# Where the modulation of layer 0's gate and of layer 1 is computed: between the blocks of layer 0's merge, or between the projections of its mLSTM stage

## The chip, the core and the metric

The kernel runs on one core of a Trainium2 chip. The metric is the device time of one execution in microseconds (us). The engines are TensorE (PE in the profile, PEld for its weight loads), VectorE (DVE), ScalarE (ACT), GpSimd (POOL) and SyncE (SP), whose queue issues all of this kernel's loads.

## The reference

Two layers of a diffusion backbone. Each layer norms its input and modulates it with shift, scale and gate, which come from a conditioning vector. It feeds the result to three token mixers and merges their outputs by gates computed from the same input.

```python
def layer_fwd(x, xc, c, c_ctx, ...):
    shift, scale, gate = jnp.split(jax.nn.silu(c) @ w_mod + b_mod, 3, axis=-1)
    shift_c, scale_c, gate_c = jnp.split(jax.nn.silu(c_ctx) @ w_mod + b_mod, 3, axis=-1)
    h = rms_norm(x, norm_g) * (1.0 + scale[:, None]) + shift[:, None]
    hc = rms_norm(xc, norm_g) * (1.0 + scale_c) + shift_c
    p = [h @ w for w in split_cols(w_in, IN_SIZES)]      # and pc from hc
    y_a = ssd_branch(...); y_b = diff_branch(...); y_c = mlstm_branch(...)
    def merge(ya, yb, yc, gates):
        g = jax.nn.sigmoid(gates).reshape(gates.shape[:-1] + (N_BRANCH, D_MODEL))
        mixed = (g[..., 0, :] * (ya @ w_branch[0]) + g[..., 1, :] * (yb @ w_branch[1])
                 + g[..., 2, :] * (yc @ w_branch[2]))
        return mixed @ w_out
    x_new = x + gate[:, None] * merge(y_a, y_b, y_c, p[13])
    xc_new = xc + gate_c * merge(yc_a, yc_b, yc_c, pc[13])
```

There are 256 latent and 256 context tokens, and D_MODEL is 1024. `w_mod` is 1024 x 3072 for each layer. All numbers are 32-bit floats.

## The kernel before

**Projections.** A weight matrix is streamed in granules of 512 rows by 256 columns (`granules`, lines 123 to 139). SP loads 512 KB into one of three `raw` buffers, ScalarE rounds it to `whi` (line 120), and VectorE subtracts to get the rest, `wlo` (line 82, called from `split`). Both have three buffers. Three products (hi x hi, hi x lo, lo x hi) add up in PSUM: `mm_tok` (lines 149 to 151, 256 columns to an instruction) for outputs in token layout, `proj_ch` (lines 180 to 182, 512 columns) for outputs in channel layout. The sums stand in three PSUM banks named `acc`. A `proj_ch` takes two of them, a `proj_tok` one for each pair of token tiles.

**Order.** The Tile framework puts each engine's instructions into an order before the kernel runs. It takes those that are ready in a simulated time line, by priority. Band 0 (loads, splits, evacuations) goes ahead of band 1 (the mixers), and that ahead of band 2 (projections, and the modulation here). Within a band the order of the program counts. On the chip every engine's order is fixed. A pool that is opened on the memory of a released pool waits for the last use of what lay there.

**Stages of a layer.** These are the norm, branch A (SSD), branch B (differential attention), branch C (mLSTM), the merge and the output projection. The mLSTM stage runs `ml_core(j)` for four heads (band 1). It is a chain over four chunks in two directions in which TensorE, ScalarE and VectorE hand small tiles to each other: `pw`, `nu` (line 1105), `dn` (lines 1106 to 1110), `kw`, `C` (line 1125). The projections `mo_proj`, `mz_proj` and `ml_proj` of this and the next heads give TensorE work between the steps. Layer 1 computes outputs for the latent tokens alone, and so has half of those projections.

**The merge** (lines 1247 to 1279) has three branches of four column blocks. Each of the twelve steps is a gate projection (`fg`, tanh into `tg`) and a branch projection (`fb`, gate times projection, added up in `mixed`). Ahead of each branch its tokens are transposed into `yh`, `yl`.

**The modulation.** Blocks 0 to 3 of layer 0 are made at the start, on TensorE. The two blocks of layer 0's gate and the six of layer 1 are made by `mod_block` (lines 266 to 307), 512 columns of `w_mod` at a time. Four loads of 512 KB go into three `wm` buffers. For each of the eight k-tiles and the two conditioning vectors there is a product and an addition: ScalarE multiplies and GpSimd adds for one vector, and for the other VectorE does both at once in five k-tiles and ScalarE with GpSimd (over `mtmp`) in two. The sums stand in `macc` (one buffer). VectorE folds the partitions by half into `modrow` (one buffer). The block's end, `tail`, is four products on TensorE into an `acc` bank (line 300) and one VectorE addition into `modc` (line 302). The list `later` holds the eight blocks. `start()` puts one block's products into the program. `background()` puts the oldest block's tail there and then starts the next. Two blocks are started ahead, and nine places between the mLSTM's parts call `background()`.

Of the kernel before, what the change touches and what calls it, by code (L numbers as in the profile page):

```python
# [10 lines left out]
F32R = mybir.dt.float32r  # L11
# [5 lines left out]
PSUM = bass.MemoryType.PSUM  # L17

D = 1024
P = 128  # L20
KT = D // P
NT = 4
# [12 lines left out]
def hybrid_backbone_kernel(ctx: ExitStack, tc: tile.TileContext, A, out, dbg=None):  # L35
# [4 lines left out]
    # ---- priority bands: 0 loads, splits and evacuations; 1 mixers; 2 projections  # L40
# [52 lines left out]
    def bc(ap, n):  # L93
        """append a broadcast free dim of n"""
        return ap.unsqueeze(len(ap.shape)).to_broadcast(list(ap.shape) + [n])

    # ---- constants
# [20 lines left out]
    # ---- weight stream: granules of 4 k-tiles by 256 columns; hi/lo split on chip  # L118
# [4 lines left out]
    def granules(srcs):  # L123
        """srcs: dram pieces [1024, n] that make 256 columns; yields (k0, hi, lo)"""
        for g in range(2):
            with band(0):
                raw = mk(wts, [P, 4, 256], "raw", bufs=3)
                c = 0
                for src in srcs:
                    n = src.shape[1]  # L130
                    nc.sync.dma_start(
                        raw[:, :, c : c + n],
                        src[g * 512 : (g + 1) * 512, :].rearrange("(k p) n -> p k n", p=P),
                    )
                    c += n
                hi = mk(wts, [P, 4, 256], "whi", F32R, bufs=3)
                lo = mk(wts, [P, 4, 256], "wlo", F32R, bufs=3)
                split(raw, hi, lo)
            yield 4 * g, hi, lo

    def mm_tok(ps, lhs, tcol, k0, hi, lo):
        """one pair of token tiles times 4 k-tiles of weights; both tiles share a bank"""
        xh, xl = lhs
        for i in range(2):
            sl = slice(tcol + i * P, tcol + (i + 1) * P)
            o = ps[:, i * 256 : (i + 1) * 256]
            for j in range(4):
                k = k0 + j
                T.matmul(o, lhsT=xh[:, k, sl], rhs=hi[:, j, :], start=(k == 0 and i == 0), stop=False)  # L149
                T.matmul(o, lhsT=xh[:, k, sl], rhs=lo[:, j, :], start=False, stop=False)  # L150
                T.matmul(o, lhsT=xl[:, k, sl], rhs=hi[:, j, :], start=False, stop=(k == KT - 1 and i == 1))  # L151

    def proj_tok(srcs, lhs, pairs, evac):
        """out[tok, 256]; a pair of token tiles per bank, evacuated as [128, 2, 256]"""
        ps = {}
        with band(2):
            for p in pairs:
                ps[p] = pacc()
        for k0, hi, lo in granules(srcs):
            with band(2):  # L160
                for p in pairs:
                    mm_tok(ps[p], lhs, p * 256, k0, hi, lo)
        for p in pairs:
            with band(0):
                evac(p, ps[p].rearrange("p (t n) -> p t n", t=2))

    def proj_ch(srcs, lhs, ranges, evac, halves=False, gr=None):
        """out[128 channels, tokens] for 2 channel tiles; ranges[i] = (tok0, tok1)"""
# [34 lines left out]
    def rsqrt(src, n, scale, eps, pp=P, pool_=True):  # L203
        """1/sqrt(src*scale+eps) for a narrow [pp, n] tile"""
# [18 lines left out]
    # ---- modulation columns of one layer: four column tiles of the array share the contraction  # L223
    def mod_pair(l, cbs, pool, bufs, rbufs, between=None, each=None, end=False):
        with band(2):
            ps = pacc()
            for x, cb in enumerate(cbs):
                if x and between:
                    between()
                for k0 in range(0, KT, 2):  # L230
# [10 lines left out]
                    for j in range(2):  # L241
                        k = k0 + j
                        g = k % 4
                        # the second block's rows lie two below the first's
                        T.matmul(
                            ps[32 * g : 32 * g + 32, :], lhsT=cst[:, k, 2 - 2 * x : 34 - 2 * x], rhs=wm[:, j, :],
                            start=(x == 0 and k < 4), stop=(x == 1 and k >= 4), skip_group_check=True,
                        )
# [17 lines left out]
    def mod_block(l, cb, pool):  # L266
        """512 columns of the modulation: multiplied and added up by k-tile, TensorE sums the partitions"""
        with band(2):
            acc = mk(pool, [P, 2, 512], "macc", bufs=1)
            for k0 in range(0, KT, 2):  # L270
# [5 lines left out]
                for j in range(2):  # L276
# [6 lines left out]
                    else:  # L283
                        if k in (1, 2, 4, 5, 7):
                            stt(acc[:, 1, :], w_, cb_, acc[:, 1, :], ALU.mult, ALU.add)
                        else:
                            t_ = mk(pool, [P, 512], "mtmp", bufs=2)
# [21 lines left out]
    # ---- narrow parameters of a layer: loads, and what is made of them  # L309
    def narrow(l, pool):  # L310
# [7 lines left out]
        gcs = mk(small, [P, 2, 2, 64], "gcs", bufs=1)  # (q|k), lat tile: cos * gain  # L318
        gsn = mk(small, [P, 2, 2, 64], "gsn", bufs=1)  # (q|k), lat tile: signed sin * swapped gain
# [16 lines left out]
        def compute():  # L336
            # scaled sign and decay columns
# [3 lines left out]
            # -lambda  # L341
# [5 lines left out]
            # rotary tables with the gains folded in; 1/sqrt(64) goes into q  # L347
# [11 lines left out]
    # ================= set-up  # L359
# [4 lines left out]
    with band(0):  # L364
# [11 lines left out]
        # small loads go between the large ones  # L376
        few = []
        for l in range(depth):
            w_ = prow[l]
            # per-channel parameters as rows: 16 for each layer  # L380
# [22 lines left out]
        # silu of the conditioning vectors, as columns  # L403
# [14 lines left out]
    def columns(l):  # L418
# [5 lines left out]
        # convolutions feed silu(x) = (x/2)(1 + tanh(x/2)): taps and bias are halved  # L424
# [8 lines left out]
    # the first weights, ahead of the second half of the modulation  # L433
# [17 lines left out]
    xcur = None  # x of the latent tiles after layer 0  # L451

    class Tokens:
        """token-layout [tokens, 1024] in slots of [128, 2 tiles, 512 columns]"""
# [4 lines left out]
        def __call__(self, b, p):  # L459
            """block of 256 columns of a pair of tiles: [128, 2, 256]"""  # L460
            return self.t[b // 2, p][:, :, (b % 2) * 256 : (b % 2 + 1) * 256]

        def tile(self, g, t):
            """half of the columns of one token tile: [128, 512]"""
            return self.t[g, t // 2][:, t % 2, :]

        def col(self, t, k):
            """[128 tokens, 128 channels]"""
            return self.tile(k // 4, t)[:, (k % 4) * P : (k % 4 + 1) * P]

    for l in range(depth):
        last = l == depth - 1
        w_in = A["w_in"][l]
        pq = (1,) if last else (0, 1)  # pairs of token tiles whose outputs are needed
# [13 lines left out]
        # ================= modulated norm -> hT (hi, lo)  # L488
# [63 lines left out]
        # ---------- pools of this layer  # L552
# [5 lines left out]
        sm = mk(mlrow, [P, 512], "sm", F32R)  # -M rows, hi over lo  # L558
        mlc = mk(mlrow, [P, 5, NT, 8], "mlc")  # w, sc, em, wk, cdec columns
        sa = mk(sp, [P, 512], "sa", F32R)  # L560
        col = mk(sp, [P, 5, NT, 2, 16], "col")  # -acs, exp(acs), dt*exp(end-acs), dt, exp(end)
# [19 lines left out]
        with band(1):  # L581
# [61 lines left out]
            # rows -> columns  # L643
# [8 lines left out]
            # per-chunk scalars on all partitions  # L652
# [32 lines left out]
        # ---------- depthwise convolution + silu of a channel tile (in PSUM) -> [128, n]  # L685
# [13 lines left out]
        # gate path: 2 silu(z) of [128, 2, 256]  # L699
# [7 lines left out]
        # ================= branch A: SSD  # L707
# [34 lines left out]
        def ssd_core(g):  # L742
            hs = slice(8 * g, 8 * g + 8)
            with band(1):
# [10 lines left out]
                # chunk states  # L755
# [70 lines left out]
        # ================= branch B: q, k, v of two heads  # L826
# [43 lines left out]
        # ================= branch B: differential attention  # L870
# [31 lines left out]
        halves_ = (slice(0, 64), slice(64, 128))  # the two maps of a head  # L902

        def attn_tr(qt, h):
            """q as hi over lo (map 1: lo over hi), k as hi over hi, and the lo of k"""
# [25 lines left out]
        def attn_head(qt, h):  # L931
# [3 lines left out]
            with band(1):  # L935
                po = pm()
                for t in tq:
# [16 lines left out]
                    # E0 - lambda (sum0 / sum1) E1; the factor 1 / sum0 joins the norm below  # L954
# [20 lines left out]
        def attn_fin(qt):  # L975
            ssB, r0B = aS[qt]
            with band(1):
                # rms over a head: r0 / sqrt(mean((r0 o)^2) + eps)
# [19 lines left out]
        # ================= branch C: projections of one mLSTM head  # L998
# [49 lines left out]
        # branch A: rms over the row  # L1048
# [16 lines left out]
        # ================= branch C: mLSTM  # L1065
# [75 lines left out]
        def mo_post(j, ths):  # L1141
            with band(1):
# [8 lines left out]
                # zz holds 2 silu(z)  # L1151
# [18 lines left out]
        later = ([] if l else [(0, 4), (0, 5)]) + ([] if last else [(l + 1, cb) for cb in range(6)])  # L1170
        tails = []

        def start():
            if later:
                tails.append(mod_block(*later.pop(0), mp_))

        def background():
            if tails:
                tails.pop(0)()
            start()  # L1180

        start()
        dz_proj(3)
        start()
# [6 lines left out]
        background()  # L1191
        ml_core(1)
        ths = mo_proj(1)
        background()
        zzs = mz_proj(1)
        background()
# [4 lines left out]
        background()  # L1201
        mo_post(2, mo_proj(2))
        background()
        mz_post(2, mz_proj(2))
        background()
        ml_core(3)
        mo_post(3, mo_proj(3))
        background()
        mz_post(3, mz_proj(3))
        while later or tails:  # L1210
            background()
# [14 lines left out]
        # ================= merge, in channel layout  # L1226
        yt_pool = tc.alloc_tile_pool(name=f"yt{l}", bufs=1, side="right")
        tg_pool = tc.alloc_tile_pool(name=f"tg{l}", bufs=1, side="right")
        mixed = []
        mT = ([], [])  # L1230
        per = D // nqt  # channel tiles in a slot of mixed
        per = 2 if nqt == 512 else 4

        def transposed(y, scale_of):
            """token layout -> (hi, lo) [128, 8, tokens], scaled by a per-channel column"""
# [11 lines left out]
        for b, (y, sc_) in enumerate(((ya, lambda k: pcol(k, 9)), (yb, lambda k: pcol(0, 11)), (yc, lambda k: pcol(k, 10)))):  # L1247
            with band(1):
                yT = transposed(y, sc_)
            for cb in range(4):  # L1250
# [28 lines left out]
                proj_ch([A["w_branch"][l, b][:, cb * 256 : (cb + 1) * 256]], yT, [(0, nqt)] * 2, fb)  # L1279

        tg_pool.release()

        # ================= output projection and residual
        ep = tc.alloc_tile_pool(name=f"out{l}", bufs=1)
        xnew = Tokens(yx, "y", pq) if not last else xcur
        with band(1):
            gbc = {}
            for p in pq:
                gbc[p] = mk(ep, [P, D], "gbc", bufs=2)
                cc = 1 - p  # L1290
                for hf in range(2):
# [3 lines left out]
                    # half of the gate: the merge gates are 1 + tanh  # L1295
# [41 lines left out]
        # the other half of the columns: weights resident, one pair of token tiles after the other  # L1337
# [79 lines left out]
```

## Time and profile before

| | us |
|---|---|
| median of 3 runs | 1770.94 |
| the runs | 1769.58, 1770.94, 1775.22 |
| span of the profiled execution | 1772.7 |
| TensorE busy | 1707.9 (96%) |
| VectorE busy | 1233.4 (70%) |
| ScalarE busy | 829.6 (47%) |
| GpSimd busy | 296.4 (17%) |

The profiled execution's own time is not listed apart from its span. The page cuts the span into forty slices of 44.3 us, and a digit is the busy share in tenths. Busy shares over the whole span are means over stages with different limits, so the tables of single stretches are what to read. Matmuls overlap, so the spacing of their starts tells their cost, not their durations. A releaser is what ended an engine's idle time.

### The profile page before, as it was taken

How to read it: one execution, taken by the hardware profiler on the slowest of the kernel's cores; microseconds unless marked ns; L12 is line 12 of the kernel's file. 1: busy time of each engine (PE TensorE's matmuls, PEld its weight loads, DVE VectorE, ACT ScalarE, POOL GpSimd, SP SyncE). 2: the span in 40 equal slices, each digit the busy share in tenths (PEclk: the TensorE clock that was granted, in tenths of full speed). 3: DMA queues.
4: the chain of work that ended last, by engine and by line, in shares of the span. 5: the costliest groups of instructions: out<-in, count | busy, mean ns of one | idle time of the engine just before them, and what ended most of it. 6: DMA issues, size and time to landing. Idle time of an engine off the chain costs nothing.

```text
span 1772.7 us, 28884 instructions
## 1 busy us (share of the span) xinstructions
PE 1707.9 (96%) x11256; PEld 1512.4 (85%) x11256; DVE 1233.4 (70%) x2279; ACT 829.6 (47%) x1609; POOL 296.4 (17%) x296
## 2 busy tenths in 40 slices
PE   5999999999999798899999999999999999999998
PEld 1787889999899687888888889888898989999998
DVE  4798887777765999973434445787887876776565
ACT  3455535554545465642323333545554555444453
POOL 1012331111000646520011000111221210000000
PEclk8999999999999898999999999999999999999999
DMA  8422112222223434423323334232232223335554
GB/s 257 120 72 65 55 60 72 62 70 61 74 60 107 132 119 143 143 62 96 96 83 95 96 119 112 67 89 84 72 120 72 84 78 114 95 97 171 177 176 143
DMA packets 192052, 180.39 MB, mean 102 GB/s; under 512 B 20750, under 2 KB 178064, under 8 KB 191916
## 3 DMA queue, kind: packets, MB, share of 16 engines
q1 hardware_dynamic: 191916, 178.54, 33.5%
q8 instruction: 89, 1.46, 0.3%
q14 instruction: 47, 0.39, 0.1%
HBM read 177.47 MB, written 1.05 MB: 101 GB/s over the span
## 4 chain that ended last, share of the span: by engine, by line
PE 55%; DVE 6%; issue 1%; ACT 1%; POOL 0%; DVEq 0%; POOLq 0%; ACTq 0%
PE acc L180 9%; PE acc L182 9%; PE acc L181 9%; PE acc L151 6%; PE acc L149 6%; PE acc L150 6%; DVE macc L79 1%; PE pm L967 1%; PE pe L949 1%; DVE dn L82 1%; PE pm L1120 1%; DVE wlo L82 1%; PE pe L948 1%; PE pm L764 1%; PE pe L1104 1%
## 5 line engine op out<-in xcount | busy, mean ns | idle before, releaser
L82 DVE TENSOR_TENSOR wlo<-raw,whi 128x1024 fp32r<-128x1024 f32 x274 | 349.5, 1276 | 263.1 <-ACT whi L120 261.5
L149 PE MATMUL acc<-whi,hh 128*128 128x256 f32 x1728 | 504.9, 292 | 7.8 <-DVE modc L82 5.1
L151 PE MATMUL acc<-whi,hl 128*128 128x256 f32 x1728 | 506.5, 293 | 0.0
L150 PE MATMUL acc<-wlo,hh 128*128 128x256 f32 x1728 | 506.3, 293 | 0.0
L120 ACT CAST whi<-raw 128x1024 fp32r<-128x1024 f32 x274 | 287.7, 1051 | 372.2 <-PE acc L181 238.4
L149 PEld LDWEIGHTS acc<-whi,hh 128*128 128x128 f32 x1728 | 333.6, 193 | 17.4 <-issue 5.7
L151 PEld LDWEIGHTS acc<-whi,hl 128*128 128x128 f32 x1728 | 333.6, 193 | 10.7 <-issue 8.8
L150 PEld LDWEIGHTS acc<-wlo,hh 128*128 128x128 f32 x1728 | 333.6, 193 | 10.6 <-issue 8.1
L180 PE MATMUL acc<-hh,whi 128*128 128x512 f32 (+1 forms) x712 | 255.2, 361 | 2.5 <-DVE zz L79 2.5
L181 PE MATMUL acc<-hl,whi 128*128 128x512 f32 (+1 forms) x712 | 254.4, 358 | 0.2 <-DVE hl L82 0.2
L182 PE MATMUL acc<-hh,wlo 128*128 128x512 f32 (+1 forms) x712 | 253.3, 357 | 0.0
L180 PEld LDWEIGHTS acc<-hh,whi 128*128 128x128 f32 x712 | 134.4, 190 | 22.6 <-DVE zz L79 2.9
L181 PEld LDWEIGHTS acc<-hl,whi 128*128 128x128 f32 x712 | 135.0, 190 | 20.4 <-issue 3.1
L182 PEld LDWEIGHTS acc<-hh,wlo 128*128 128x128 f32 x712 | 135.0, 190 | 19.0 <-issue 1.2
L181 PE MATMUL acc<-yl,whi 128*128 128x512 f32 (+1 forms) x384 | 129.4, 339 | 0.0
L180 PE MATMUL acc<-yh,whi 128*128 128x512 f32 (+1 forms) x384 | 129.2, 339 | 0.0
L182 PE MATMUL acc<-yh,wlo 128*128 128x512 f32 (+1 forms) x384 | 128.9, 338 | 0.0
L82 POOL TENSOR_TENSOR macc<-macc,wm 128x512 f32<-128x512 f32 x56 | 81.3, 1452 | 116.6 <-ACT wm L290 106.4
L951 DVE TENSOR_REDUCE nmax<-pe 128x1 f32<-128x512 f32 (+1 forms) x96 | 56.3, 598 | 34.9 <-PE pe L949 33.7
L181 PEld LDWEIGHTS acc<-yl,whi 128*128 128x128 f32 x384 | 72.1, 188 | 8.5
L182 PEld LDWEIGHTS acc<-yh,wlo 128*128 128x128 f32 x384 | 71.9, 188 | 8.6
L180 PEld LDWEIGHTS acc<-yh,whi 128*128 128x128 f32 x384 | 72.0, 188 | 8.4
(310 smaller groups left out, 2848.8 us busy)
## 6 DMA issues: line engine op xcount, KB each, us to landing
raw<-in_w_in_dram SPq DMA_DIRECT2D x192, 512.0 KB
raw<-in_w_branch_dram SPq DMA_DIRECT2D x48, 512.0 KB
wm<-in_w_mod_dram SPq DMA_DIRECT2D x45, 512.0 KB
raw<-in_w_in_dram SPq DMA_DIRECT2D x48, 256.0 KB
raw<-in_w_out_dram SPq DMA_DIRECT2D x16, 512.0 KB
raw<-in_w_mod_dram SPq DMA_DIRECT2D x3, 512.0 KB
xin<-in_ctx_dram SPq DMA_DIRECT2D x2, 512.0 KB
xin<-in_x_dram SPq DMA_DIRECT2D x2, 512.0 KB
```

The lines of the kernel that those rows point to most:

```text
L79: (eng or V).scalar_tensor_tensor(out=o, in0=a, scalar=s, in1=b, op0=op0, op1=op1)
L82: (eng or V).tensor_tensor(out=o, in0=a, in1=b, op=op)
L120: S.copy(hi, raw)
L149: T.matmul(o, lhsT=xh[:, k, sl], rhs=hi[:, j, :], start=(k == 0 and i == 0), stop=False)
L150: T.matmul(o, lhsT=xh[:, k, sl], rhs=lo[:, j, :], start=False, stop=False)
L151: T.matmul(o, lhsT=xl[:, k, sl], rhs=hi[:, j, :], start=False, stop=(k == KT - 1 and i == 1))
L180: T.matmul(o, lhsT=hi[:, j, cs], rhs=xh[:, k, a:b], start=(k == 0 and first), stop=False)
L181: T.matmul(o, lhsT=hi[:, j, cs], rhs=xl[:, k, a:b], start=False, stop=False)
L182: T.matmul(o, lhsT=lo[:, j, cs], rhs=xh[:, k, a:b], start=False, stop=(k == KT - 1 and final))
L764: T.matmul(pt, lhsT=BT[:, c, :], rhs=xw, start=True, stop=True)
L948: T.matmul(o, lhsT=q2[m][:, qs], rhs=k2[m][:, 0:N], start=True, stop=False)
L951: V.tensor_reduce(out=ng[:, m : m + 1], in_=es[m][0], axis=AX.X, op=ALU.max, negate=True)
```

## The change

`start`, `background`, `later` and `tails` move from the mLSTM stage to the merge. The blocks' tiles are taken from a pool of their own, `bg`, which is opened after the mLSTM's pools and those of layer 1's narrow parameters are released, and closed after the merge's loop. One block is started ahead of the merge, in place of two, and `background()` is called once after each of the twelve steps. `mtmp` takes its two buffers from the pool `ev` under the tag `zz`, which has the same size and is the mLSTM's gate tile otherwise. Comments and docstrings go, which changes nothing that runs.

```diff
@@ -284,7 +284,7 @@
                         else:
-                            t_ = mk(pool, [P, 512], "mtmp", bufs=2)
+                            t_ = mk(ev, [P, 512], "zz", bufs=2)
                             S.mul(t_, w_, cb_)
@@ -1167,48 +1167,25 @@
-        later = ([] if l else [(0, 4), (0, 5)]) + ([] if last else [(l + 1, cb) for cb in range(6)])
-        tails = []
-
-        def start():
-            if later:
-                tails.append(mod_block(*later.pop(0), mp_))
-
-        def background():
-            if tails:
-                tails.pop(0)()
-            start()
-
-        start()
         dz_proj(3)
-        start()
         ths = mo_proj(0)
         zzs = mz_proj(0)
         ml_core(0)
         mo_post(0, ths)
         mz_post(0, zzs)
         mls[2] = ml_proj(2)
-        background()
         ml_core(1)
         ths = mo_proj(1)
-        background()
         zzs = mz_proj(1)
-        background()
         ml_core(2)
         mo_post(1, ths)
         mz_post(1, zzs)
         mls[3] = ml_proj(3)
-        background()
         mo_post(2, mo_proj(2))
-        background()
         mz_post(2, mz_proj(2))
-        background()
         ml_core(3)
         mo_post(3, mo_proj(3))
-        background()
         mz_post(3, mz_proj(3))
-        while later or tails:
-            background()
         mp_.release()
         mlin.release()
@@ -1223,16 +1200,31 @@
         yt_pool = tc.alloc_tile_pool(name=f"yt{l}", bufs=1, side="right")
         tg_pool = tc.alloc_tile_pool(name=f"tg{l}", bufs=1, side="right")
+
+        bg = tc.alloc_tile_pool(name=f"bg{l}", bufs=1)
+        later = ([] if l else [(0, 4), (0, 5)]) + ([] if last else [(l + 1, cb) for cb in range(6)])
+        tails = []
+
+        def start():
+            if later:
+                tails.append(mod_block(*later.pop(0), bg))
+
+        def background():
+            if tails:
+                tails.pop(0)()
+            start()
+
+        start()
         mixed = []
@@ -1277,10 +1269,14 @@
                 proj_ch([A["w_branch"][l, b][:, cb * 256 : (cb + 1) * 256]], yT, [(0, nqt)] * 2, fb)
-
+                background()
+        while later or tails:
+            background()
+
+        bg.release()
         tg_pool.release()
```

## Rows read from the trace of the kernel before

**Rows 1.** The page: the span, and busy tenths in 40 slices.
```profile
span 1772.7 us, 28884 instructions
...
PE   5999999999999798899999999999999999999998
...
DVE  4798887777765999973434445787887876776565
...
POOL 1012331111000646520011000111221210000000
PEclk8999999999999898999999999999999999999999
```
**Rows 2.** Table of stretches: length, busy us (instructions) by engine, clock, DMA share, GB/s.
```profile
core 0: us, PE busy (x) PEld busy (x) DVE busy (x) ACT busy (x) POOL busy (x), PEclk, DMA share, GB/s
570.00:770.00 200.00, 170.64 (x1070) 154.66 (x1069) 189.93 (x353) 111.11 (x217) 110.39 (x80) 0.91 0.44 134
780.00:980.00 200.00, 200.00 (x921) 164.41 (x920) 79.57 (x97) 60.59 (x86) 11.51 (x10) 1.00 0.29 90
1500.00:1590.00 90.00, 90.00 (x631) 84.46 (x630) 65.69 (x175) 41.34 (x87) 3.37 (x8) 1.00 0.33 98
1590.00:1710.00 120.00, 120.00 (x1011) 119.73 (x1010) 70.99 (x98) 58.52 (x91) 6.65 (x10) 1.00 0.56 173
```
**Rows 3.** Waits of PE, 560 to 790 us: us in total, times, longest.
```profile
PE pm L1099 <- ACT nu L1101: 6.1, 4, 2.9
PE pe L1104 <- DVE C L79: 5.3, 5, 2.5
PE acc L149 <- DVE modc L82: 5.1, 1, 5.1
```
**Rows 4.** Table of stretches, one slowed slice of the mLSTM stage.
```profile
610.00:620.00 10.00, 4.85 (x23) 4.83 (x23) 8.99 (x14) 2.54 (x4) 7.22 (x5) 0.54 0.54 155
```
**Rows 5.** Timeline of PE: start us, us, instruction; 512-column matmuls at both clocks.
```profile
584.87 0.63 PE L181 MATMUL acc<-hl,whi 128*128 128x512 f32 x1
585.30 0.63 PE L182 MATMUL acc<-hh,wlo 128*128 128x512 f32 x1
...
780.84 0.40 PE L182 MATMUL acc<-hh,wlo 128*128 128x512 f32 x1
...
782.22 0.39 PE L182 MATMUL acc<-hh,wlo 128*128 128x512 f32 x1
```
**Rows 6.** Tile macc, then wm, 570 to 785 us; durations ns min/median/max, first and last start.
```profile
570.00:785.00 215.00, 55.18 (x64) 5.81 (x8) 104.41 (x72) 0.92 0.43 130
570.00:785.00 215.00, 0.00 (x0) 0.00 (x0) 42.23 (x48) 56.49 (x80) 81.30 (x56) 0.92 0.43 130
...
L82 POOL TENSOR_TENSOR macc<-macc,wm x56: 1261/1296/2237, 576.5 to 763.7; 128x512 f32<-128x512 f32 x56
L82 DVE TENSOR_TENSOR modrow<-macc x16: 686/689/1667, 593.0 to 767.7; 64x512 f32<-64x512 f32 x16
L273 SPq DMA_DIRECT2D wm<-in_w_mod_dram x32: 367/368/547, 568.6 to 749.3; - x32
```
**Rows 7.** Groups, 565 to 780 us, then layer 1's 1500 to 1590 us: busy us, mean ns.
```profile
L82 DVE TENSOR_TENSOR dn<-dn,nu 128x1 f32<-128x1 f32 x30 | 14.5, 483 | 0.4
...
L82 DVE TENSOR_TENSOR dn<-dn,nu 128x1 f32<-128x1 f32 x14 | 2.2, 154 | 0.2
```
**Rows 8.** Waits of SP's queue, 560 to 790 us, then 790 to 980 us.
```profile
SPq L273 <- POOL macc L82: 92.7, 26, 10.5
...
SPq L131 <- DVE wlo L82: 166.1, 32, 7.2
```
**Rows 9.** Tile raw, 780 to 1000 us: the splits on VectorE.
```profile
L82 DVE TENSOR_TENSOR wlo<-raw,whi x37: 1210/1225/2361, 779.9 to 995.6; 128x1024 fp32r<-128x1024 f32 x37
```

## The prediction

> **What bounds the kernel now.** I read the page first: the span is 1772.7 us, and its forty slices show where TensorE is not simply busy at full clock [rows 1]. Slices 14 to 17, in the mLSTM stage of layer 0, are the only stretch away from the two ends in which TensorE stands at 7 or 8 tenths; slice 14 has the only clock mark under 9 there; VectorE stands at 9 in all four, and GpSimd is busier than in any other stage. The second view is the table of stages [rows 2]. From 570 to 770 us TensorE is busy 170.64 of 200 us, so 29.4 us are idle; VectorE is busy 189.93 us (95%); the granted clock is 0.91. In the merge that follows (780 to 980 us) TensorE has no idle time at clock 1.00, while VectorE is busy 79.57 of 200, ScalarE 60.59 and GpSimd 11.51. So the kernel is bound by TensorE nearly everywhere, and in this one stage by a VectorE that cannot serve TensorE in time. The list of TensorE's waits in that stage says on whom it waits [rows 3]: on VectorE's and ScalarE's steps of the mLSTM core (C, nu), and 5.1 us on `modc`, the last step of a modulation block, which holds one of the three `acc` banks.
>
> The clock is a second loss. A slice such as 610 to 620 us has 4.85 us of matmuls and a granted clock of 0.54 [rows 4]. What that costs is seen in the order of time [rows 5]: matmuls of 512 columns start 0.43 us apart at the low level, 1.2 GHz (584.87 and 585.30 us, behind a wait), and 0.23 us apart at 2.4 GHz (780.84 to 782.22 us, six steps). A mean clock of 0.91 over 200 us means 18 us of full-clock work not done, if TensorE had been busy throughout; it was busy about 65% of its time in the slowed slices, which gives 12 us. So the stage loses 29.4 + 12 to 18 = **41 to 47 us** against TensorE's own work; I take 44.
>
> **The change part by part.** *What leaves the mLSTM stage.* Eight blocks of modulation, together [rows 6] 55.2 us of VectorE (64 instructions), 56.5 us of ScalarE (80), 104.4 us of GpSimd (72) and 32 loads of 512 KB. On VectorE 189.9 - 55.2 = 135 us stay. A further part of VectorE's time goes too: with GpSimd adding beside it, the 128x1 `dn` product takes 483 ns, and in layer 1's mLSTM, which has no modulation, 154 ns [rows 7]. So 30 of them hold 9.9 us of mere waiting, and other groups of the stage are stretched likewise. VectorE then has at most 135 us to do in some 156 us (200 - 44), and probably 105 to 115. Layer 1's mLSTM shows what that load permits: 65.69 of 90 us of VectorE (73%), TensorE 90.00 of 90 at clock 1.00 [rows 2]. It runs the same core with only half of the outputs, and so with less projection work to fill gaps. I therefore take a residue of 2 us; its bounds are 0 (layer 1's row) and 8 (VectorE at 135 of 156).
>
> *TensorE's work itself* is unchanged. The 64 small matmuls of the blocks' ends move along. They were paid in the sum of TensorE's work before and are paid after.
>
> *What arrives in the merge.* The merge runs twelve steps, each a gate and a branch projection of 48 matmuls of 512 columns: 96 x 0.23 = 22 us. After each step comes one block's end and the start of the next, so eight steps, 176 us, carry the modulation. Per block: GpSimd 9 x 1.30 = 11.7 us (104.4 / 8 = 13.1 with the waits of before), ScalarE 10 x 0.71 = 7.1, VectorE 55.2 / 8 = 6.9 at the most [rows 6]. Per step of 22 us VectorE has 79.57 / 200 x 22 = 8.8 us now and would have 15.7 (71%); ScalarE 6.7 + 7.1 = 13.8 (63%); GpSimd some 14 (64%). Each stays under its step. The loads come to 16.8 MB over 176 us, 95 GB/s beside the 90 that are there: 185. Layer 1's merge (1590 to 1710 us) runs at 173 GB/s with VectorE 59% and ScalarE 49% busy, and TensorE has no idle time there [rows 2]. That is the nearest row for the merge after the change, and it says the arrival is free.
>
> *SP's queue.* The 32 loads and their waits move past the merge's weight loads. In the mLSTM stage SP sat 92.7 us in 26 waits for GpSimd to give back a `wm` buffer, the longest 10.5 us; in the merge it sits 166.1 us waiting for `raw` buffers [rows 8]. Weight loads queue behind a modulation load that waits. The cover: three `raw` buffers, each one granule of 24 x 0.23 = 5.5 us of TensorE, 16.5 us in all, besides the split ones. 10.5 is under 16.5, so nothing; without that cover see the second rival.
>
> *The banks.* Between two steps the block's end takes one of three `acc` banks, so the next gate projection needs the bank that the branch projection has just left. Its first half ends 12 x 0.23 = 2.8 us before the step does, so VectorE has that long, plus the block's end, to read it. A split on VectorE normally takes 1.23 us there, at the worst 2.36 [rows 9]. Bounds: 0 to 8 x 2.4 = 19 us (one full hold each time); I take 3, nearer to the median than to the worst. *The first block* waits for the memory of the mLSTM pools and of layer 1's narrow parameters, so its end may come later than the first step's: 0 to 10 us, taken as 1, since TensorE can take the next projection first.
>
> A rule of the Trainium skill speaks against the change here. The rows show that `dn` is held by GpSimd's adds [rows 7] and that a split has a worst case of 2361 ns beside a median of 1225 [rows 9]. The page "SBUF — State Buffer", section "Who interferes with whom", says that a VectorE instruction with two SBUF inputs and a GpSimd instruction that reads SBUF exclude each other, the later one waiting for the whole of the other. The split's subtraction is of that kind, so by the rule the 72 adds now meet the weight splits. By the rule's worst case each of the four splits of a step waits one add, 4 x 1.3 = 5 us of VectorE, which then stands at 94% of the step; by layer 1's row nothing is late. The trace agrees with the rule as far as `dn` goes.
>
> **Sum.** -44 + 2 + 3 + 1 = -38 us against the span of 1772.7, that is 1734.7. The profiled execution's own time is not listed. Its span lies 1.8 us above the median of the three runs and inside their range, so I take the same from the result: **1733 us**, 2.1% faster. Its own range is 1771 - 47 to 1771 - 23, the latter with half of the banks' bound and the full residue: 1724 to 1748.
>
> **The rivals.**
> *The mLSTM core, not the modulation, holds the stage.* TensorE's waits name C and nu of the core [rows 3], a chain from TensorE to VectorE and back, which would remain. If half of the loss stays, the gain is 44 / 2 - 4 = 18: 1753 us. Against it stands layer 1's stage with no idle time. Chance 0.10.
>
> *SP's queue ties the merge to the modulation (slower).* `macc` and `modrow` have one buffer each and `wm` has three, while a block needs four loads. The fourth can wait until GpSimd starts the next block, and that waits for the previous block's end on TensorE. If SP's order puts it ahead of weights that TensorE needs, the wait is a block's whole pace, 174.7 / 7 = 25 us before [rows 6], against 16.5 us of cover: 8.5 us idle each time, and 13 with the clock's share (15 on 29 us of idle time, as above). It turns the sign when three or more of the seven later blocks do so (38 / 13); with five, 1733 + 65 = 1798 us. For it: 26 of 32 loads did wait. Against: the longest wait was 10.5 us, with VectorE twice as loaded as it would be. Chance 0.07.
>
> *The port and the banks.* By the mechanism weighed above, a VectorE held by GpSimd reads banks late at each of the eight ends: 19 us in place of 3, and with half as much again for the clock 1733 + 16 + 9 = 1758 us. For it: `dn`; against it: VectorE has idle time left. Chance 0.08.
>
> *No change*, because one of these takes back the whole gain: 1771 us, chance 0.05. That the blocks don't move at all is hardly possible, as their memory is that of the mLSTM pools.
>
> **How the numbers follow.** Forecast 0.70 (1724 to 1748), core 0.10 (1753), port and banks 0.08 (1758), none 0.05, slower 0.07. The range that holds 8 in 10 takes in the first two and a little below the forecast's best: 1721 to 1757. A measurement of this kernel tells about 0.3% (5.3 us) from no change. Below 1766 lie the first three: 0.88; within 0.05; above 0.07.
>
> **What would show it.** In the profile after, layer 0's mLSTM stage should take about 155 to 160 us for the same matmuls, with TensorE busy throughout, clock 1.00 and `dn` near 155 ns. The merge should last as before (some 265 us), with VectorE at 60 to 75% of it, GpSimd at half, DMA near 185 GB/s, and TensorE's waits under 5 us. Idle time before L180 in the merge that names `modc`, `y` or `tg` on VectorE speaks for the banks; one that names whi or wlo behind raw loads speaks for SP; idle time before L1099 and L1104 in the mLSTM stage speaks for the core. The prediction is wrong if the merge shows clock losses of its own.

## The result: 20 us faster, where 38 were forecast

The changed kernel takes 1750.8 us (median of four runs, 1749.97 to 1752.11) against 1770.9 before: a ratio of 0.9882, with a 95% interval of 0.9868 to 0.9896. The forecast was 1733 us with a range of 1721 to 1757. The sign and the range held; the gain was half of the forecast's. The span of its profile lies 1.8 us below that execution's time. If that holds for before as well, its profile (span 1772.7) is that of a somewhat longer execution of about 1774.5; the two spans differ by 4 us more than the medians do. Of e12_before_no_gpsimd below, the profiled execution was a slow one (1859 us), so its trace isn't read and its time is that of the other three.

The table of stretches of the changed kernel answers to [rows 2]; the columns are the same (the last two rows are the stretch around two of the waits below).

```profile
570.00:740.00 170.00, 169.93 (x1149) 157.87 (x1155) 112.65 (x318) 69.93 (x155) 3.83 (x8) 1.00 0.25 71
740.00:960.00 220.00, 202.67 (x927) 166.16 (x926) 155.42 (x153) 110.86 (x158) 122.17 (x82) 0.96 0.50 153
...
750.00:760.00 10.00, 8.08 (x34) 6.45 (x34) 8.57 (x10) 3.92 (x6) 6.85 (x5) 0.83 0.50 132
760.00:770.00 10.00, 6.50 (x26) 5.44 (x27) 7.27 (x10) 4.17 (x7) 5.94 (x5) 0.83 0.63 203
```

The first row is the mLSTM stage: TensorE idle for 0.07 of 170 us, clock 1.00, VectorE at 66%. All that was to be gained there was gained. The second is the merge, which had neither idle time nor clock loss before. Now 17.3 us are idle, and a clock of 0.96 over 220 us costs another 8 (220 x 0.04 x 92% busy). That is the missing part. The list of TensorE's waits (560 to 1060 us; us in total, times, longest) says on whom:

```profile
PE acc L180 <- DVE y L79: 6.0, 2, 5.0
PE acc L300 <- DVE modrow L82: 4.5, 1, 4.5
PE acc L180 <- DVE tg L79: 3.5, 3, 1.6
PE pm L1233 <- DVE yl L79: 3.2, 1, 3.2
```

Two of the four belong to the first block: its end in TensorE's queue waits 4.5 us for `modrow`, and the transposes wait 3.2 us for `yl`, queued on VectorE behind the first block and the mLSTM's last products. The other two, 9.5 us, are gate projections that wait for VectorE to read a bank. What VectorE was doing stands in the groups (740 to 925 us), which answer to [rows 7, 9]:

```profile
L79 DVE SCALAR_TENSOR_TENSOR macc<-wm,cst,macc 128x512 f32<-128x512 f32 x40 | 52.0, 1300 | 20.0 <-POOL macc L82 19.6
L82 DVE TENSOR_TENSOR wlo<-raw,whi 128x1024 fp32r<-128x1024 f32 x27 | 47.8, 1771 | 20.1 <-ACT whi L120 19.3 <-DVE modrow L82 0.2
L79 DVE SCALAR_TENSOR_TENSOR y<-tg,acc 128x512 f32<-128x512 f32 x8 | 5.3, 678 | 1.0 <-PE acc L182 1.0
```

The same read of a bank in the kernel before (790 to 960 us):

```profile
L79 DVE SCALAR_TENSOR_TENSOR y<-tg,acc 128x512 f32<-128x512 f32 x8 | 5.5, 687 | 13.4 <-PE acc L182 13.4
```

An addition to `macc` takes 1300 ns on the mean and a split 1771, where the splits in the merge of before (790 to 960 us) had a mean of 1334 and a median of 1225 [rows 9]; and VectorE waits 19.6 us for GpSimd at `macc`. The read of a bank itself (`y`) takes 678 ns, and took 687 before: it is late, not slow. How one wait of 5 us comes about is in the order of time:

```profile
812.72 1.74 DVE L79 SCALAR_TENSOR_TENSOR macc<-wm,cst,macc 128x512 f32<-128x512 f32 x1 [2.44 <-POOL macc L82]
814.49 0.72 ACT L290 ACTIVATE wm<-wm,cst 128x512 f32<-128x512 f32 x1 [2.80 <-DVE macc L79]
815.12 1.03 ACT L120 CAST whi<-raw 128x1024 fp32r<-128x1024 f32 x1
816.18 1.82 DVE L82 TENSOR_TENSOR wlo<-raw,whi 128x1024 fp32r<-128x1024 f32 x1 [1.72 <-ACT whi L120]
817.93 1.27 DVE L79 SCALAR_TENSOR_TENSOR y<-tg,acc 128x512 f32<-128x512 f32 x2
818.66 0.80 PE L180 MATMUL acc<-hh,whi 128*128 128x512 f32 x1 [5.00 <-DVE y L79]
```

The end of an addition on GpSimd lets VectorE's go at 812.72, and that takes 1.74 us. ScalarE's product waits for it, the cast of a weight granule is queued behind that product, the split behind the cast, and the read of the bank behind the split. The list names only the last link.

### The profile page after: what moved, and what is told of

The parts are those of the page before. It is cut to its first block, busy times and chain, and to the rows that moved or that the text cites. A ratio compares the mean times of both kernels' runs of the same rounds, so it can differ in the third digit from the quotient of the medians.

```text
span 1748.2 us, 28875 instructions
## 1 busy us (share of the span) xinstructions
PE 1695.7 (97%) x11240; PEld 1504.4 (86%) x11256; DVE 1224.0 (70%) x2279; ACT 831.4 (48%) x1609; POOL 300.3 (17%) x296
## 5 line engine op out<-in xcount | busy, mean ns | idle before, releaser
L82 DVE TENSOR_TENSOR wlo<-raw,whi 128x1024 fp32r<-128x1024 f32 x274 | 359.5, 1312 | 218.5 <-ACT whi L120 216.5
L150 PEld LDWEIGHTS acc<-wlo,hh 128*128 128x128 f32 x1728 | 329.8, 191 | 10.8 <-issue 8.1
L151 PEld LDWEIGHTS acc<-whi,hl 128*128 128x128 f32 x1728 | 329.8, 191 | 10.4 <-issue 8.5
L149 PEld LDWEIGHTS acc<-whi,hh 128*128 128x128 f32 x1728 | 329.8, 191 | 8.6 <-issue 5.4
L82 POOL TENSOR_TENSOR macc<-macc,wm 128x512 f32<-128x512 f32 x56 | 88.7, 1585 | 36.9 <-issue 17.7
```

Source lines behind the costliest of these rows:

```text
L82: (eng or V).tensor_tensor(out=o, in0=a, in1=b, op=op)
```

## The experiments

After this reading there were four theories of the 25 us that the merge lost. *Bank*: the block's end takes the third `acc` bank. *Hand-over*: VectorE waits for GpSimd's part of the same sum, and what is queued behind it is late. *Port*: GpSimd's additions stretch VectorE's instructions that run beside them. *First block*: it starts and ends too early. The kernels of one set ran on one chip beside the kernel before; ratios are to that. There were three sets: e1 to e4; the yardstick, e5, e6 and e9; e10 to e14. The kernel before had medians of 1773.5, 1770.2 and 1771.2 us in them, so a difference of times between two sets is good to some 3 us.

**The yardstick.** The changed kernel again.

> The changed kernel itself, unaltered, as the yardstick of this set of runs: 1750 to 1753 us, with the same four waits of TensorE in the merge (17 us) by every theory.

Measured: 1752.4 us, ratio 0.9893 (0.9870 to 0.9917), with the same four waits, 16.6 us in all.

**The bank.**

```diff
         def tail():
             with band(2):
-                pc = pacc()
+                pc = pe()
```

> The changed kernel with the ends of the modulation blocks put into a bank of the group pe instead of acc; nothing else. Bank theory (TensorE waits in the merge because the block's end takes the third acc bank, so that the next gate projection needs the one just left): the 9.5 us of waits of L180 on VectorE's y and tg vanish, with half as much again for the clock, so 1750.8 - 14 = about 1737 us. Hand-over theory (VectorE is late because its fixed order puts modulation work that waits for GpSimd ahead of its reads): the read is as late as before, and one more bank covers it only in part: 1743 to 1751. Port theory (VectorE is stretched by GpSimd's adds until it is late): as hand-over, 1743 to 1751. In all three the mean of VectorE's additions to macc stays near 1300 ns.

Measured: 1742.8 us, ratio 0.983 (0.9793 to 0.9867). The waits on `y` stay at 5.4 us, three times, so the bank theory's main term, 9.5 us on `y` and `tg`, falls only to 6.3 (0.9 of it on ScalarE's `tg`). The wait of TensorE for `modrow` is gone, which no theory had: the edit also gives TensorE another order. The gain of some 10 us is about what that wait, the 3 us on `tg` and the clock behind them can have cost; which part is whose this run doesn't show.

**Every block's end one step later**, the first block's above all.

```diff
-                background()
+                if b or cb:
+                    background()
```

> The changed kernel without the call of background() after the very first step, so every block's end stands one step later in the program. All theories: the 4.5 us wait of TensorE for modrow at the first end goes, with 2 us for the clock: about 1744. If the other waits only move on by a step, no more than that; if the modulation's slack of one more step also removes the waits on y and tg, 1737 or lower, which would speak for the hand-over theory and against the bank theory.

Measured: 1738.9 us, ratio 0.982 (0.9777 to 0.9863), 13.5 us better than the yardstick, more than was expected of that one wait. Its waits of TensorE (560 to 1060 us) and its table:

```profile
PE acc L180 <- DVE y L79: 3.9, 4, 2.4
PE acc L180 <- DVE tg L79: 2.7, 2, 1.6
PE pm L1233 <- DVE yl L79: 0.8, 1, 0.8
```

```profile
740.00:960.00 220.00, 212.37 (x974) 173.78 (x973) 161.56 (x159) 113.93 (x160) 123.26 (x82) 0.98 0.51 157
```

`modrow` is gone from the list, `yl` falls from 3.2 to 0.8, and the clock of the stretch rises from 0.96 to 0.98; `y` and `tg` keep 6.6 of 9.5 us. So the first block's waits, with the clock behind them, are the greater part of the 13.5 us. VectorE's additions (1318 ns) and its waits for GpSimd at `macc` (19.6 us) are as in the change.

**No hand-over.**

```diff
-                        if k in (1, 2, 4, 5, 7):
+                        if k:
                             stt(acc[:, 1, :], w_, cb_, acc[:, 1, :], ALU.mult, ALU.add)
```

> The changed kernel with the second vector's sum made by VectorE alone: in k-tiles 3 and 6 it multiplies and adds at once as in the other five, and the 16 ScalarE products and 16 GpSimd additions over zz go. The other 56 GpSimd additions stay. Hand-over theory: VectorE's 19.6 us of waits on GpSimd at macc vanish, and with them the waits of L180 on y and tg, some 9.5 + 5 us: about 1737. Port theory: 56 of 72 additions still hold VectorE, which has 16 instructions of 0.75 to 1.7 us more: 1745 to 1755. Bank theory: VectorE's reads are a little earlier, 1745 to 1751.

Measured: 1740.4 us, ratio 0.9817 (0.9784 to 0.985). VectorE no longer waits for GpSimd at `macc`. TensorE's waits on `y` and `tg` fall from 9.5 to 3.2 us, but `yl` (3.8) and `modrow` (2.7) stay, and VectorE's additions still take 1235 ns. The edit also takes 16 of GpSimd's 72 additions and 16 products of ScalarE, so it doesn't set the hand-over apart from the stretching; the time lies between what the two theories expected.

**Without GpSimd's additions** (the sum of the first vector over the k-tiles, and two k-tiles of the second, are left out).

```diff
-                            tt(acc[:, 1, :], acc[:, 1, :], t_, ALU.add, eng=G)
...
-                        tt(acc[:, 0, :], acc[:, 0, :], w_, ALU.add, eng=G)
```

> The changed kernel without any of GpSimd's 72 additions to macc, so the modulation is incomplete: it leaves out the sum over k-tiles of the first vector and two of the second. ScalarE's products, VectorE's additions, the loads and the blocks' ends stay. Port theory: VectorE's additions to macc fall from 1300 ns to 750 and the splits from 1771 ns to 1230, and all waits of TensorE in the merge but the first block's go: about 1735. Hand-over theory: the same time, since there is nothing left to wait for, about 1735; the difference from e3_one_engine is then what the port alone costs (near 0 by the hand-over theory, 10 or more by the port theory). Bank theory: waits on y and tg stay, 1745 to 1751.

Measured: 1729.1 us, ratio 0.9756 (0.9722 to 0.979). One wait of 1.9 us (`yl`) is left. The groups (740 to 960 us) show what let go:

```profile
L82 DVE TENSOR_TENSOR wlo<-raw,whi 128x1024 fp32r<-128x1024 f32 x36 | 45.2, 1256 | 54.8 <-ACT whi L120 53.9
L79 DVE SCALAR_TENSOR_TENSOR macc<-wm,cst,macc 128x512 f32<-128x512 f32 x40 | 30.0, 750 | 13.0 <-DMA wm<-in_w_mod_dram 12.0
```

Additions at 750 ns in place of 1300 and splits at 1256 in place of 1771, with the blocks' ends still in `acc`. Loads, ScalarE's products and the remaining additions cost the merge next to nothing (1.9 us idle, clock 0.99). The first block's end doesn't wait either, although it stands where it stood in the change: `modrow` is ready at 754.1 us and TensorE comes to the end at 757.7, where in the change TensorE comes at 759.0 and `modrow` is ready at 763.4. Both the stretching and the hand-over are gone here, so this run says what GpSimd's additions cost, not by which of the two.

**The same cut in the kernel before** (the same sums left out; blocks between the mLSTM's projections).

> The kernel before the change, without any of GpSimd's 72 additions to macc: it leaves out the sum over k-tiles of the first vector and two of the second; the blocks stay in the mLSTM stage. It tells what of the stage's loss of 41 to 47 us GpSimd causes. If VectorE's volume is the cause (55 us of modulation in a stage of 200), it still has 39 us of the blocks' work: half of the loss stays, about 1750 us. If the stretching by GpSimd is the cause (dn 483 ns against 154, additions 960 against 750), dn is back at 155 ns and most of the idle time is gone: 1730 to 1738 us.

Measured: 1732.2 us, ratio 0.9785 (0.9757 to 0.9814). Table of stretches, then a group of 565 to 760 us, against [rows 2, 7]:

```profile
570.00:770.00 200.00, 195.71 (x1307) 178.41 (x1306) 159.50 (x410) 126.76 (x249) 5.18 (x10) 1.00 0.48 148
```

```profile
L82 DVE TENSOR_TENSOR dn<-dn,nu 128x1 f32<-128x1 f32 x32 | 4.9, 154 | 0.4
```

In the old place, with VectorE's 45 us of the blocks still there, TensorE idles 4.3 us in place of 29.4, at full clock. VectorE's busy time in the same 200 us falls from 189.93 to 159.50 us, with more instructions (410 in place of 353). It had hardly waited for GpSimd there: before, from 570 to 785 us, its waits at `macc` were

```profile
DVE macc L79 <- POOL macc L82: 1.2, 1, 1.2
```

So it was GpSimd's additions that made the mLSTM stage slow: by stretching VectorE's instructions, more than by what VectorE itself had to add.

**Everything on VectorE** (complete sums).

```diff
-                        S.mul(w_, w_, ca_)
-                        tt(acc[:, 0, :], acc[:, 0, :], w_, ALU.add, eng=G)
+                        stt(acc[:, 0, :], w_, ca_, acc[:, 0, :], ALU.mult, ALU.add)
```

together with the edit of e3_one_engine.

> The changed kernel with both sums made by VectorE, multiplied and added at once, complete; no ScalarE product and no GpSimd addition is left in the loop but the first. VectorE has 14 x 0.75 + 2 x 0.69 + 0.48 = 12.4 us of work for a block in place of 10.9 us stretched (6.5 + 0.5 + 1.9, and 2 on four splits). Port theory: nothing is stretched any more (0.75 us an addition, 1.25 us a split), TensorE's waits in the merge fall under 5 us: about 1733 us. Hand-over theory: the same, as no engine waits for another within a block. Volume theory (VectorE has simply too much to do for its reads to be in time): VectorE is no less busy, so waits on y and tg stay near 9 us: 1743 to 1751.

Measured: 1740.5 us, ratio 0.982 (0.9794 to 0.9847). Its list of TensorE's waits (560 to 1060 us), and its table for the merge and around the first block:

```profile
PE acc L299 <- DVE modrow L82: 4.9, 1, 4.9
PE pm L1232 <- DVE yl L79: 2.1, 1, 2.1
```

```profile
740.00:960.00 220.00, 213.01 (x990) 175.81 (x989) 165.57 (x230) 68.01 (x91) 11.54 (x10) 0.97 0.53 158
750.00:765.00 15.00, 10.11 (x43) 8.42 (x44) 14.10 (x21) 1.77 (x2) 0.00 (x0) 0.73 0.55 159
765.00:780.00 15.00, 15.00 (x55) 12.11 (x56) 14.73 (x24) 3.91 (x5) 0.00 (x0) 0.82 0.72 203
```

Not one wait on `y` or `tg`, though VectorE is busier than in the change (165.57 of 220 us against 155.42) and the ends take an `acc` bank. That speaks against volume in the merge, and against the bank as a cause by itself. The waits are 7.0 us, yet the median missed its 1733 by 7 (the profiled execution, 1735.9, by 3). The two rows of 15 us hold both of the low clock's stretches. Taken in steps of half a us, the granted clock is 0.50 from 750.0 to 753.0, behind the 2.1 us on `yl`, and again from 760.5 to 770.0, from within the 4.9 us on `modrow` until 7 us after it; between and behind them it is 1.00.

**The three edits e1, e2 and e3 together.**

> The three edits together: the blocks' ends in a bank of pe, the first of them a step later, and the second vector's sum on VectorE alone. If each took away its own part (modrow 4.5 us, banks, hand-over), their gains add up as far as the sum of 17 us of waits and 8 us of clock goes: 1750.8 - 20 = about 1731 us, near the 1729 without any addition on GpSimd. If the port is what is left (VectorE's additions stay near 1250 ns and splits near 1640 ns), some 5 us of waits on y and yl stay: 1735 to 1738.

Measured: 1729.3 us, ratio 0.9761 (0.9738 to 0.9784), the waits 3.0 us. Its row of the merge and its groups:

```profile
740.00:960.00 220.00, 217.08 (x1031) 178.71 (x1031) 186.14 (x185) 106.53 (x153) 108.69 (x66) 1.00 0.53 165
```

```profile
L79 DVE SCALAR_TENSOR_TENSOR macc<-wm,cst,macc 128x512 f32<-128x512 f32 x56 | 68.8, 1228 | 1.4
L82 DVE TENSOR_TENSOR wlo<-raw,whi 128x1024 fp32r<-128x1024 f32 x35 | 63.0, 1804 | 15.0 <-ACT whi L120 14.1
```

That is 23 us of what the change lost, although additions (1228 ns) and splits (1804) are as stretched as ever and VectorE stands at 85%. So the stretching costs little here once a step and a bank cover the late reads and the second sum waits for no other engine.

**e5_three without the edit of e3.**

> The changed kernel with the blocks' ends in a bank of pe and the first of them a step later; both sums as in the change, on VectorE, ScalarE and GpSimd. It is e5_three without the move of the second vector's sum. If the hand-over from GpSimd to VectorE is a cause of its own: 1735 to 1740 us, with 5 us or more of waits on y and tg. If start and banks are all there is: 1729 to 1732 us.

Measured: 1733.0 us, ratio 0.9781 (0.9763 to 0.98). The waits are 4.4 us (`yl` 2.6, `y` 1.8), with 5.6 us left of VectorE's waits for GpSimd. It lies between the two expectations, and its interval overlaps that of e5_three. Whether the hand-over costs anything beside the stretching, once the first end and the bank are moved, these runs don't tell.

**e5_three with the first vector on VectorE too**, so without GpSimd.

> The changed kernel with both sums on VectorE, the blocks' ends in a bank of pe and the first of them a step later. It differs from e5_three only in that the first vector's 56 additions leave GpSimd. Port theory: with nothing stretched it is a little faster than the 1729 of e5_three, 1725 to 1729 us. If e5_three has already all that is to be had: 1728 to 1731 us.

Measured: 1726.0 us, ratio 0.9745 (0.9721 to 0.9768), as the port theory had it; the difference from e5_three is within the intervals.

**The first block after the first step in the program, sums on VectorE, ends in `acc`.** e9_no_gpsimd with one line less.

```diff
-        start()
         mixed = []
```

> The changed kernel with both sums on VectorE (as e9_no_gpsimd) and without the call of start() ahead of the merge, so that the first block starts after the first step and ends after the second; the ends stay in an acc bank. What e9_no_gpsimd had left was the first block alone: 2.1 us on yl and 4.9 us on modrow, with the clock at 0.73 and 0.82 for 30 us behind it. If the first block's place is the cause, all of it goes: 1740.5 - 7 - 6 = 1725 to 1729 us, with under 2 us of waits in the merge. If the banks matter without GpSimd too, 1732 or more.

Measured: 1724.5 us, ratio 0.9734 (0.9716 to 0.9753): the lowest median (e10_no_gpsimd_late_bank's interval overlaps), 26 us better than the change and 46 better than before. Its table of stretches and the group of VectorE's additions:

```profile
570.00:740.00 170.00, 169.93 (x1148) 157.81 (x1154) 112.53 (x320) 69.90 (x156) 3.83 (x8) 1.00 0.25 70
740.00:960.00 220.00, 220.00 (x1045) 182.21 (x1045) 170.31 (x235) 72.11 (x97) 11.49 (x10) 1.00 0.54 165
```

```profile
L79 DVE SCALAR_TENSOR_TENSOR macc<-wm,cst,macc 128x512 f32<-128x512 f32 x112 | 76.8, 746 | 0.2
```

TensorE has no idle time in the merge, at clock 1.00, with VectorE at 77%. Against e9_no_gpsimd the one call is worth 16 us by the medians; between the two profiled executions it is 12.2 us, of which 7.0 are the waits and the rest is about what the low clock took. The trace also says what moved. On the chip the first block starts when it did (742.5 us, 741.9 in e9_no_gpsimd) and its `modrow` is ready when it was (762.9 and 763.1); its end on TensorE stands at 776.6 us in place of 763.1. So the first block didn't start too early: TensorE met its end too early, before the sum was made.

**The old place with everything on VectorE** (complete sums).

> The kernel before the change, with both sums made by VectorE, multiplied and added at once, complete, and nothing on GpSimd; the blocks stay in the mLSTM stage. Port theory alone (GpSimd's additions caused the stage's whole loss): near the 1732 us without additions, 1732 to 1742. Volume theory (the place matters, since VectorE has no room there): VectorE has 115 us of the stage's own work (159.5 of 200 us without additions, less 45 of the blocks) and 99 us of blocks, 214 us where TensorE has 167: the stage is as long as before, 1762 to 1778 us.

Measured: 1751.5 us (1750.9 to 1754.9), ratio 0.989 (0.9866 to 0.9914). Both expectations missed. It is 19 us faster than before, so GpSimd was not needed there either; and it is 27 us slower than the same sums in the merge (e14_later_start; 11 slower than e9_no_gpsimd), so the place does matter once VectorE has 99 us to add. The stage is shorter than a sum of VectorE's work (214 us) had it; why is not shown.

## Why the prediction was half right

The measured 1750.8 us lies 3 us outside the forecast's own 1724 to 1748. The wider range held because it took in the rival of the mLSTM core at 1753 us, whose mechanism the first row of the result excludes; that part is luck.

- **What left the mLSTM stage: right.** The step took 44 us (41 to 47) for the loss and 2 for a residue. The stage has no idle time and full clock. e14_later_start, where the merge loses nothing, is 46 us faster than before: the upper end of the term. The reading of *why* was too simple, though: the prediction put the loss down to a VectorE with too much to do, 55 us of modulation and 10 or more of waiting. e6_before_no_adds shows that what GpSimd's additions stretched was the greater part. (On the page of before, slice 16 has a clock mark of 8 too, and slice 15 stands at 9 tenths; no sum rests on either.)
- **What arrives in the merge: the step that failed.** The busy shares were near what was worked out for a step: in 740 to 925 us VectorE stood at 76% (71% over the 220 us) for 71%, GpSimd at 65% for 64%. From them and layer 1's merge the step concluded that the arrival is free. But layer 1's merge has 6.65 us of GpSimd in 120 [rows 2], so it is no row for a merge in which GpSimd adds for half of the time. Loads were indeed free (e4_no_adds), and so was the volume on VectorE once the first end stood a step later (e14_later_start); GpSimd's additions beside VectorE were not: without them 17.3 us of idle time became 1.9 (e4_no_adds).
- **The banks and the port: mechanism right in part, term mis-sized.** 3 us were taken of 0 to 19; the waits on `y` and `tg` measured 9.5, and more with the clock. The bound assumed one hold of a split; the trace shows a chain of five instructions on VectorE and ScalarE, begun by a wait for GpSimd. The rival with the port and the banks at 1758 us is closer in mechanism and 7 us off in time (its 9 us for the clock is 1 more than half of its 16). How much of the 9.5 us is stretching and how much waiting for GpSimd's part of the sum stays open. The Trainium skill's page "SBUF — State Buffer" ("Who interferes with whom") has it that a VectorE instruction with two SBUF inputs contends with a GpSimd instruction that reads SBUF, while one with at most one SBUF input, outside the 2-port performance modes, does not. The trace agrees on both sides: additions 1300 against 746 to 750 ns, splits 1771 against 1222 to 1256, and the bank's read, one of whose inputs is in PSUM, 678 against 687 ns.
- **The first block: mis-sized.** 1 us was taken because TensorE could take the next projection first. It could not: its order had the end ahead. 4.5 us, 3.2 more on `yl`, which the prediction did not have, and the clock behind both made most of the 13 us of e2_late_tail, and 12 to 16 in the pair e9 and e14. The place alone did not cost it: with part of the sums left out the end does not wait at the same place (e4_no_adds), with all of them on VectorE it does (e9_no_gpsimd).
- **The clock in the merge** has no term in the sum. The rivals priced it at half of a wait, and the last line named it as a sign of being wrong. It cost 8 us of the 25.
- **SP's queue:** the rival did not come. SP's waits for GpSimd there sum to 63.4 us with a longest of 4.8, under the cover of 16.5, and TensorE's list of waits in the merge names no weight load.
- **The core as the bound:** excluded by the first row of the result.

## What to carry to other kernels

Work that is moved into a stage without idle time has to be priced by what it puts *ahead* of the reads that free buffers, on every engine's fixed order, and not by busy shares: VectorE at 71% with GpSimd beside it was late at the banks, at 77% with hardly anything on GpSimd it was not (e14_later_start), and at 85% with GpSimd beside it but a step and a bank more it hardly was (e5_three). A stage taken as proof that there is room must have the same mix of engines busy. And the first use of a moved pipeline deserves its own look: one step more between its start and its end was worth 12 to 16 us.

## What the runs showed of the hardware

- A 128x512 addition on GpSimd that runs beside VectorE takes the latter's addition from 746 ns (e14_later_start) to a mean of 1300 and a 128x1024 split from 1222 to 1771. Giving GpSimd 72 additions therefore relieved VectorE of little: with all of them back on it, its busy time in the same 220 us rises only from 155 to 166 or 170 us, and the kernel is 12 us faster (e9_no_gpsimd against after_again).
- An idle gap's length alone did not settle what became of the clock. In e9_no_gpsimd TensorE idled 2.10 us and then ran at 1.2 GHz (granted clock 0.50) for 3 us; in e5_three it idled 2.10 us, for `yl` as well, and the granted clock of that row stayed at 1.00. A gap of 1.93 us in e4_no_adds was followed by 3 us at 0.50.

```profile
749.99 1.11 PE L1232 MATMUL pm<-ident,yb 128*128 128x128 f32 x4 [2.10 <-DVE yl L79]
```

```profile
PE pm L1233 <- DVE yl L79: 2.1, 1, 2.1
```

```profile
750.00:765.00 15.00, 12.90 (x61) 10.31 (x60) 14.66 (x16) 6.61 (x10) 9.14 (x7) 1.00 0.56 152
```

The first line is of e9_no_gpsimd's order of time; the others are e5_three's waits and its table of stretches.
